# First feed-forward product with both parts of the activations in one 512-column matmul

## The chip, the cores and the metric

The kernel runs on one core of one Trainium2 chip. A core has a matrix engine (TensorE; PE in the profile, its weight loads PEld), a vector engine (VectorE, DVE), an activation engine (ScalarE, ACT), GpSimd (POOL) and a queue that issues DMA transfers (SyncE, SP). The metric is the device time of one launch in microseconds (us). Matmuls write to PSUM, which is divided into banks of 512 float32 columns on 128 partitions.

## The reference

Two layers over 256 tokens of width 1024. Each layer normalises its input, runs three token mixers and adds their gated sum; then comes the feed-forward block, which is what this case is about:

```python
def hybrid_layer(x, ...):
    h = rms_norm(x, g_mix)
    z = h @ w_in
    ...
    x = x + (g_a * o_a + g_b * o_b + g_c * o_c) @ w_out
    h = rms_norm(x, g_ffn)
    x = x + jnp.square(jax.nn.relu(h @ w_ff1)) @ w_ff2
    return x
```

`w_ff1` is 1024 x 4096 and `w_ff2` 4096 x 1024, all in float32.

## The kernel before

**Products in three parts.** A float32 number is split exactly into two float32r numbers, a high and a low part. A product is then three float32r matmuls that add up in PSUM: high by high, high by low and low by high. Weights arrive by DMA in pieces of 128x1024 into one of five `raw` buffers; `piece` (L153, L154) splits a piece: ScalarE copies `raw` to `hi`, VectorE subtracts and writes `lo`. There are four `hi` and four `lo` buffers; the second feed-forward product takes its pieces (named `hi2`, `lo2`) from a second ring of five larger buffers.

**The feed-forward block.** It goes in 16 groups per layer, each with 256 of the 4096 hidden channels: two halves u = 0, 1 of 128 channels. `ff1(gi)` loads and splits two pieces of `w_ff1`, one for each half. `gemm_b` (L163 to L165) then makes, for each half and each of 8 row tiles k of 128 input channels, three matmuls of 256 columns (the 256 tokens): `hi` by `h2`, `hi` by `l2`, `lo` by `h2`, where `h2` and `l2` are the high and low parts of the transposed, scaled input. Both halves lie side by side in one PSUM bank. The pool `mm` has two banks, so two groups can be under way. Then ScalarE takes the relu out of the bank (L888), squares it into `rh` (L890), VectorE computes the same square with full precision (L891) and subtracts to get the low part `rl` (L892).

`acc_pass` makes the second product: for each group 24 matmuls of 512 columns (L171 to L173, tiles `f`) into four banks that hold the sums of the whole layer. In program text the first product of group gi + 1 stands ahead of the second product of group gi; the second products of the last three groups are held back to the end of the layer.

**The start of the block.** `transposed` (L203 to L208) turns the residual stream into `h2` and `l2`, 128x128 chunk by chunk: TensorE transposes (`n2t`), ScalarE scales into `h2` (L207), VectorE subtracts into `l2` (L208). The first group takes the row tiles k in two halves, 0 to 3 and 4 to 7, in the order in which they arrive.

**What sets the order.** The order on each engine is decided when the program is built: a scheduler orders the instructions by priority (the order of the text, corrected by hand in places) and by when it expects their inputs and buffers to be ready. On the chip each engine works through its own list in that order, and an instruction that has to wait holds up everything behind it on its engine.

Of the kernel before, what the change touches and what calls it, by code (L numbers as in the profile page):

```python
# [8 lines left out]
F32 = mybir.dt.float32  # L9
# [7 lines left out]
P = 128  # L17
# [14 lines left out]
# column offsets of the packed per-partition parameters  # L32
# [9 lines left out]
# row-broadcast gains of the rotary dims: [g, g with halves swapped]  # L42
# [16 lines left out]
# w_in: columns read with tokens on the output's partitions, then those with channels there  # L59
# [6 lines left out]
# the mixers' steps in the order of their data, and by urgency  # L66
# [19 lines left out]
def trunk_kernel(ctx: ExitStack, tc: tile.TileContext, A, out, depth=DEPTH):  # L86
# [54 lines left out]
    def piece(src, k, ring=0, half=0):  # L141
        """a piece [128, k, n] of a weight, split exactly into two float32r parts"""
        n = src.shape[-1]
        r = raw(src, n)
        if ring == 0:
            hi = wp.tile([P, 1024], R32, tag="hi", name="hi", bufs=WB)[:, :n]
            lo = wp.tile([P, 1024], R32, tag="lo", name="lo", bufs=WB)[:, :n]
        else:
            if half == 0:
                ring2[0] = (ap_.tile([P, 2048], R32, tag="big", name="hi2", bufs=BIG),  # L150
                            ap_.tile([P, 2048], R32, tag="big", name="lo2", bufs=BIG))
            hi, lo = (t[:, half * 1024:half * 1024 + n] for t in ring2[0])
        act(hi, r, AF.Copy)  # L153
        tt(out=lo, in0=r, in1=hi.bitcast(F32), op=ALU.subtract)  # L154
        return tuple(t.rearrange("p (k n) -> p k n", k=k) for t in (hi, lo))
# [3 lines left out]
    def gemm_b(ps, wh, wl, ah, al, ks, first=True, last=True):  # L159
        """ps[channel, token] += w^T a^T"""  # L160
# [5 lines left out]

    def gemm_a(ps, ah, al, wh, wl, ks, first=True, last=True):
        """ps[token, channel] += a w"""
# [10 lines left out]
    def rsqrt(v, p, n, name):  # L179
        """1/sqrt(v) of a positive [p, n] tile"""  # L180
# [18 lines left out]
    def transposed(src, b, g, hh, hl, name, c0):  # L199
        """columns c0 ... c0 + 3 (of 128) of src [128 tokens, 1024] -> block b of (src^T * g), split"""  # L200
# [3 lines left out]
        for c in range(c0, c0 + 4):  # L204
            pc = pt[:, (c - c0) * P:(c - c0 + 1) * P]
            hc = hh[:, c, b * P:(b + 1) * P]
            act(hc, pc, AF.Copy, scale=g[:, c:c + 1])  # L207
            stt(out=hl[:, c, b * P:(b + 1) * P], in0=pc, scalar=g[:, c:c + 1], in1=hc.bitcast(F32),  # L208
                op0=ALU.mult, op1=ALU.subtract)
# [5 lines left out]
    def normed(src, b, r, grow, hh, hl, name):  # L215
        """src [128 tokens, 1024] -> columns of block b of (src * r * g)^T, split"""
# [10 lines left out]
    def sumsq_row(b, name, v):  # L227
        """mean square of x's rows in block b, plus eps"""
# [11 lines left out]
    def rope(X, n, half, ct, st, name, eng=None):  # L240
        """rotate the first 2*half columns of X [p, n, d] in place; ct, st [p, 2*half]"""
# [12 lines left out]
    def layer(l):  # L254
# [20 lines left out]

        hB = lambda t: (lambda k: t[k] if isinstance(t, list) else t[:, k, :])
# [4 lines left out]
        hh = ap_.tile([P, 8, T], R32, tag="hh", name="hh", bufs=2)  # L281
        hl = ap_.tile([P, 8, T], R32, tag="hl", name="hl", bufs=2)
        grow = raw(bass.AP(tensor=A["gmix"].tensor, offset=A["gmix"].offset + l * D, ap=[[0, P], [1, D]]), D)
        vs = stat(2, "n1v")
        for b in range(NB):
            now = tc.cur_priority
            if l > 0 and b == 0:
                # block 0 goes before the last products of the block 1 of the layer before
# [11 lines left out]
        # rotary tables times the gains of the rotated dims  # L300
# [20 lines left out]
        def part_a(i):  # L321
            """accumulators and weights; the products are added block by block"""
# [9 lines left out]
        # channel-major part  # L332
        def take(*names):
            """one or two tiles, in one bank"""
# [21 lines left out]
        def a_products():  # L356
            """the first two parts; block 0 goes ahead"""
# [70 lines left out]
        def compress_kv():  # L428
# [13 lines left out]
            for xi, (wn, pe, w2) in enumerate((("ck1", "pek", "ck2"), ("cv1", "pev", "cv2"))):  # L442
# [11 lines left out]
                # four column groups of the array at a time; their sums are added by the next product  # L454
# [41 lines left out]
        def compress_scores():  # L496
            """all heads at once: order (block, pair, group, position)"""
# [31 lines left out]
        oh = ol = None  # L529

        def softmax_unit(pS, n, gate, name):
            """pS [128, n, keys] scores, a bank -> P^T [128 keys, 4 x 128 queries]"""
# [5 lines left out]
            # the negated masked scores and their minimum  # L538
# [24 lines left out]
        def nsa_attention(jp, o):  # L563
            """heads 2 jp, 2 jp + 1 of both groups"""
            po = psum("po", "nO")

            for b, js in ((0, (0, 1)), (1, (0,)), (1, (1,))):
# [3 lines left out]
                # the groups' products take turns: halves of the array that work at the same time  # L571
# [26 lines left out]
        def mla_attention(jp, o):  # L598
            """heads 4 jp ... 4 jp + 3"""
# [35 lines left out]
        def gemm32(ps, b, w, ks, c0, n):  # L635
            """ps[token, channel] = c_q or c_kv times w, a plain float32 product"""
# [6 lines left out]
        def low_rank_norm():  # L643
# [7 lines left out]
            # eps * (mean(c_q^2) + eps): per-token scale that the norm of c_q moves into the heads' norm  # L651
# [9 lines left out]
        def rotary_keys():  # L661
            krs = stat(2, "krs")
            # rotary part of the keys, shared by the heads
# [155 lines left out]
        def gated(m, c2):  # L819
            """column tiles 2 c2, 2 c2 + 1 of mixer m's projection, gated; the last of the three sums them"""  # L820
# [12 lines left out]
            if len(done[c2]) == 3:  # L833
                if mh is None:
                    mh = ap_.tile([P, 8, T], R32, tag="hh", name="mh", bufs=2)
                    ml = ap_.tile([P, 8, T], R32, tag="hl", name="ml", bufs=2)
                c = 2 * c2
                split(mh[:, c:c + 2].rearrange("p c t -> p (c t)"), ml[:, c:c + 2].rearrange("p c t -> p (c t)"), g)

        oh = ap_.tile([P, 8, T], R32, tag="hh", name="oh", bufs=2)  # L840
        ol = ap_.tile([P, 8, T], R32, tag="hl", name="ol", bufs=2)
# [11 lines left out]
        def acc_pass(po4, held, ah, al, nk, b, ns=(0, 1)):  # L853
            """add the products of the held row tiles to the accumulators of token block b"""
# [7 lines left out]
        h2 = ap_.tile([P, 8, T], R32, tag="hh", name="h2", bufs=2)  # L862
        l2 = ap_.tile([P, 8, T], R32, tag="hl", name="l2", bufs=2)
        for b in range(NB):
            if b == 0:
                acc_pass(po4, held, mh, ml, 8, b)
            for n in range(2):
# [4 lines left out]
                transposed(x[:, b], b, K("gffn"), h2, l2, "n2t", 4 * n)  # L872
# [5 lines left out]
        def ff1(gi):  # L878
            ps = psum("mm", "ff1")
            ws = [piece(A["ff1"][l, 2 * gi + u], 8) for u in range(2)]  # L880
            # the first group takes the channels in the order in which they arrive
            for k0, k1 in ((0, 4), (4, 8)) if gi == 0 else ((0, 8),):
                for u in range(2):
                    wh, wl = ws[u]
                    gemm_b(ps[:, u * T:(u + 1) * T], lambda k: wh[:, k, :], lambda k: wl[:, k, :], hB(h2), hB(l2),
                           [(k, k) for k in range(k0, k1)], first=(k0 == 0 and (u == 0 or gi > 0)), last=(k1 == 8 and (u == 1 or gi > 0)))
            r = s2([P, 512], "r")
            act(r, ps, AF.Relu)  # L888
            rhf, rlf = pa("rh", R32), pa("rl", R32)
            act(rhf, r, AF.Square)  # L890
            stt(out=r, in0=ps, scalar=0.0, in1=r, op0=ALU.max, op1=ALU.mult)  # L891
# [38 lines left out]
def _lay(w, k, n):  # L930
    """[L, k*128, c*n] -> [L, c, 128, k*n]: chunks of n columns, contiguous per partition"""
# [4 lines left out]
def _rowsplit(w, k):  # L936
    """[L, K, n] -> [L, K/(128 k), 128, k*n]: chunks of k row tiles"""
# [118 lines left out]
```

## Time and profile before

| what | value |
|---|---|
| time, median of 3 runs | 940.52 us (935.05 to 941.61) |
| span of the profiled execution | 932.9 us |
| the profiled execution's own time | not listed apart; the three runs lie 2.2 to 8.7 us above its span |
| TensorE busy | 907.7 us, 97% of the span |
| VectorE, ScalarE busy | 642.6 us (69%), 538.4 us (58%) |
| mean granted TensorE clock | 0.996 of full speed |
| feed-forward block, layer 1 and layer 2 | about 292 to 475 us and 747 to 930 us of the span |

The span runs from the first to the last instruction of one execution that the hardware profiler recorded. The duration of a single matmul in it (283 ns for 256 columns) is longer than the distance from one start to the next, because matmuls overlap; what a stream of them costs is read from the starts. The granted clock is given as a share of full speed: 1.00 is 2.4 GHz and 0.50 is 1.2 GHz.

### The profile page before, as it was taken

What the parts mean: (1) busy time and instruction counts of PE and PEld (TensorE: products, weight loads), DVE (VectorE), ACT (ScalarE), POOL (GpSimd) and SP (SyncE); (2) the same over time, 40 slices, a digit from 0 to 9 for tenths busy, and PEclk for the clock granted to TensorE, in tenths of its full rate; (3) what the DMA queues carried; (4) which work ended last, traced back from release to release, by engine and by line L of the source; (5) the groups of instructions that cost most, each with busy time, mean ns of one, the idle gap of its engine ahead of it and who ended that gap; (6) DMA issues with size and microseconds to landing.
All of it is one profiled execution on the core that took longest, in us unless ns stands there. A gap on an engine that the chain in (4) does not pass through costs nothing.

```text
span 932.9 us, 16104 instructions
## 1 busy us (share of the span) xinstructions
PE 907.7 (97%) x6214; PEld 804.6 (86%) x6214; DVE 642.6 (69%) x1431; ACT 538.4 (58%) x987; POOL 26.8 (3%) x80
## 2 busy tenths in 40 slices
PE   3999999999999999999999999999999999999998
PEld 3899888689989899999878988877999799999996
DVE  4589899775687655555476989979657785555552
ACT  3566656897456644444245575769865575444430
POOL 3210000000000000000001000000000000000000
PEclk9899999999999999999999999999999999999999
DMA  5644732224565665555444453225435476555521
GB/s 197 250 158 137 239 119 79 77 105 167 173 208 178 233 196 188 184 194 185 125 153 171 159 199 135 85 80 178 142 104 190 155 267 207 184 188 189 186 91 46
DMA packets 43133, 151.55 MB, mean 162 GB/s; under 512 B 4784, under 2 KB 5680, under 8 KB 43056
## 3 DMA queue, kind: packets, MB, share of 16 engines
q1 hardware_dynamic: 43056, 150.52, 48.2%
q8 instruction: 49, 0.80, 0.3%
q14 instruction: 28, 0.23, 0.1%
HBM read 149.45 MB, written 1.05 MB: 161 GB/s over the span
## 4 chain that ended last, share of the span: by engine, by line
PE 89%; DVE 4%; DMA 3%; ACT 2%; POOL 1%; issue 1%; SPq 0%; DVEq 0%; ACTq 0%
PE psB L163 7%; PE psB L165 7%; PE psB L164 7%; PE f L173 6%; PE f L171 6%; PE f L172 6%; PE ff L164 6%; PE ff L163 6%; PE ff L165 6%; PE wo L164 3%; PE wo L163 3%; PE wo L165 2%; PE nS L576 2%; DVE lo L154 2%; PE psA L172 2%; PE psA L171 2%
## 5 line engine op out<-in xcount | busy, mean ns | idle before, releaser
L154 DVE TENSOR_TENSOR lo<-raw,hi 128x1024 fp32r<-128x1024 f32 (+1 forms) x266 | 317.5, 1209 | 179.0 <-ACT hi L153 140.8
L153 ACT ACTIVATE hi<-raw 128x1024 fp32r<-128x1024 f32 (+1 forms) x266 | 274.7, 1048 | 267.2 <-DMA raw<-in_ff_dram 93.6
L163 PE MATMUL psB<-hh,hi 128*128 128x256 f32 x592 | 172.4, 292 | 1.4 <-ACT ug L749 1.4
L165 PE MATMUL psB<-hh,lo 128*128 128x256 f32 x592 | 170.2, 289 | 0.0
L164 PE MATMUL psB<-hl,hi 128*128 128x256 f32 x592 | 169.5, 287 | 0.0
L165 PE MATMUL ff<-h,lo 128*128 128x256 f32 x512 | 144.5, 283 | 0.0
L163 PE MATMUL ff<-h,hi 128*128 128x256 f32 x512 | 144.5, 283 | 0.0
L164 PE MATMUL ff<-l,hi 128*128 128x256 f32 x512 | 144.3, 283 | 0.0
L163 PEld LDWEIGHTS psB<-hh,hi 128*128 128x128 f32 x592 | 113.1, 191 | 8.2 <-issue 4.4
L165 PEld LDWEIGHTS psB<-hh,lo 128*128 128x128 f32 x592 | 112.8, 191 | 3.0 <-issue 2.6
L164 PEld LDWEIGHTS psB<-hl,hi 128*128 128x128 f32 x592 | 113.1, 191 | 0.3
L758 DVE SCALAR_TENSOR_TENSOR ca<-upad,cols,ca 128x256 f32<-128x256 f32 x240 | 103.6, 477 | 0.4
L173 PE MATMUL f<-hi,rl 128*128 128x512 f32 x256 | 101.2, 395 | 0.5 <-DVE rl L892 0.5
L171 PE MATMUL f<-hi,rh 128*128 128x512 f32 x256 | 101.1, 395 | 0.0
L172 PE MATMUL f<-lo,rh 128*128 128x512 f32 x256 | 101.0, 395 | 0.0
L164 PEld LDWEIGHTS ff<-l,hi 128*128 128x128 f32 x512 | 98.0, 192 | 1.1
L163 PEld LDWEIGHTS ff<-h,hi 128*128 128x128 f32 x512 | 97.9, 191 | 1.2
L165 PEld LDWEIGHTS ff<-h,lo 128*128 128x128 f32 x512 | 98.0, 192 | 0.0
L173 PEld LDWEIGHTS f<-hi,rl 128*128 128x128 f32 x256 | 48.0, 188 | 13.0 <-DVE rl L892 1.6
L171 PEld LDWEIGHTS f<-hi,rh 128*128 128x128 f32 x256 | 48.1, 188 | 10.2
L172 PEld LDWEIGHTS f<-lo,rh 128*128 128x128 f32 x256 | 48.0, 188 | 10.3
L171 PE MATMUL psA<-hi,hh 128*128 128x512 f32 (+1 forms) x96 | 36.4, 381 | 6.9 <-ACT hi L153 6.9
(279 smaller groups left out, 1425.1 us busy)
## 6 DMA issues: line engine op xcount, KB each, us to landing
raw<-in_ff_dram SPq DMA_DIRECT2D x128, 512.0 KB, 4.0
raw<-in_wB_dram SPq DMA_DIRECT2D x74, 512.0 KB, 4.0
raw<-in_wA_dram SPq DMA_DIRECT2D x16, 512.0 KB, 4.4
raw<-in_w_out_dram SPq DMA_DIRECT2D x16, 512.0 KB, 3.5
raw<-in_wo_nsa_dram SPq DMA_DIRECT2D x8, 512.0 KB, 4.8
raw<-in_wo_mla_dram SPq DMA_DIRECT2D x8, 512.0 KB, 4.0
raw<-in_wconv_dram SPq DMA_DIRECT2D x8, 512.0 KB, 3.7
raw<-in_wA_dram SPq DMA_DIRECT2D x8, 312.0 KB, 5.3
```

The costliest lines, as they stand in the source:

```text
L153: act(hi, r, AF.Copy)
L154: tt(out=lo, in0=r, in1=hi.bitcast(F32), op=ALU.subtract)
L163: mm(ps, lhsT=wh(kw), rhs=ah(ka), start=(first and i == 0), stop=False)
L164: mm(ps, lhsT=wh(kw), rhs=al(ka), start=False, stop=False)
L165: mm(ps, lhsT=wl(kw), rhs=ah(ka), start=False, stop=(last and i == n - 1))
L171: mm(ps, lhsT=ah(ka), rhs=wh(kw), start=(first and i == 0), stop=False)
L172: mm(ps, lhsT=ah(ka), rhs=wl(kw), start=False, stop=False)
L173: mm(ps, lhsT=al(ka), rhs=wh(kw), start=False, stop=(last and i == n - 1))
L576: mm(pS[g].rearrange("p (h z k) -> p h z k", h=nj, z=2)[:, i], lhsT=qTn[gs, 2 * jp + j, b * P:(b + 1) * P], rhs=kTn[gs, :, 0:nk], start=Tr ...
L758: stt(out=ca[:, i], in0=upad[:, i, k:k + T], scalar=K("wdw", 31 * i + k), in1=ca[:, i], op0=ALU.mult, op1=ALU.add)
```

## The change

`h2` and `l2` become one tile `h2` of shape [128, 8, 2, 256], so that for each row tile the high and the low part lie side by side as 512 columns (the other activation tiles get the same layout, and are read as before). A new function `gemm_p` makes two matmuls for each row tile where `gemm_b` made three: `hi` by both parts in one matmul of 512 columns, and `lo` by the high part with 256 columns, which adds into the left half of the result. A half of a group now fills a whole PSUM bank: the left 256 columns hold hi by high plus lo by high, the right 256 columns hi by low. So one group takes both banks of the pool `mm`. The left and right columns are summed afterwards: ScalarE copies the left ones to `r`, VectorE adds the right ones, once for each half; the relu and the square follow on VectorE from `r`, and ScalarE copies the square into `rh`. The comments that the diff also drops are not shown.

```diff
+    def gemm_p(ps, wh, wl, a, ks, first=True, last=True):
+
+        n = len(ks)
+        for i, (kw, ka) in enumerate(ks):
+            mm(ps, lhsT=wh(kw), rhs=a[:, ka].rearrange("p s t -> p (s t)"), start=(first and i == 0), stop=False)
+            mm(ps[:, :T], lhsT=wl(kw), rhs=a[:, ka, 0], start=False, stop=(last and i == n - 1))
+
...
-            hc = hh[:, c, b * P:(b + 1) * P]
+            hc = h[:, c, 0, b * P:(b + 1) * P]
             act(hc, pc, AF.Copy, scale=g[:, c:c + 1])
-            stt(out=hl[:, c, b * P:(b + 1) * P], in0=pc, scalar=g[:, c:c + 1], in1=hc.bitcast(F32),
+            stt(out=h[:, c, 1, b * P:(b + 1) * P], in0=pc, scalar=g[:, c:c + 1], in1=hc.bitcast(F32),
                 op0=ALU.mult, op1=ALU.subtract)
...
+        def pair(name):
+
+            return ap_.tile([P, 8, 2, T], R32, tag="hp", name=name, bufs=2)
+
...
-        h2 = ap_.tile([P, 8, T], R32, tag="hh", name="h2", bufs=2)
-        l2 = ap_.tile([P, 8, T], R32, tag="hl", name="l2", bufs=2)
+        h2 = pair("h2")
...
         def ff1(gi):
-            ps = psum("mm", "ff1")
             ws = [piece(A["ff1"][l, 2 * gi + u], 8) for u in range(2)]
-            # the first group takes the channels in the order in which they arrive
+            pss = [psum("mm", "ff1") for _ in range(2)]
+
             for k0, k1 in ((0, 4), (4, 8)) if gi == 0 else ((0, 8),):
                 for u in range(2):
                     wh, wl = ws[u]
-                    gemm_b(ps[:, u * T:(u + 1) * T], lambda k: wh[:, k, :], lambda k: wl[:, k, :], hB(h2), hB(l2),
-                           [(k, k) for k in range(k0, k1)], first=(k0 == 0 and (u == 0 or gi > 0)), last=(k1 == 8 and (u == 1 or gi > 0)))
+                    gemm_p(pss[u], lambda k: wh[:, k, :], lambda k: wl[:, k, :], h2,
+                           [(k, k) for k in range(k0, k1)], first=(k0 == 0), last=(k1 == 8))
             r = s2([P, 512], "r")
-            act(r, ps, AF.Relu)
+            for u in range(2):
+                rt = r[:, u * T:(u + 1) * T]
+                act(rt, pss[u][:, :T], AF.Copy)
+                tt(out=rt, in0=pss[u][:, T:], in1=rt, op=ALU.add)
             rhf, rlf = pa("rh", R32), pa("rl", R32)
-            act(rhf, r, AF.Square)
-            stt(out=r, in0=ps, scalar=0.0, in1=r, op0=ALU.max, op1=ALU.mult)
+            stt(out=r, in0=r, scalar=0.0, in1=r, op0=ALU.max, op1=ALU.mult)
+            act(rhf, r, AF.Copy)
             tt(out=rlf, in0=r, in1=rhf.bitcast(F32), op=ALU.subtract)
```

The built order moves at the start of each layer's feed-forward block. The lists below are of layer 1; layer 2 has the same pattern. A row gives the line, the operation, the tile written, the tiles read and the shape; the numbers tell buffers of one name apart.

TensorE before, in the second half of group 0 (`ff1_3484`, weights `hi_3487` and `hi_3493`); `ff1_3570` is group 1:

```order
L163 MATMUL ff1_3484<-h2_3326,hi_3487 128x256
L163 MATMUL ff1_3570<-h2_3326,hi_3573 128x256
L164 MATMUL ff1_3570<-l2_3327,hi_3573 128x256
L165 MATMUL ff1_3570<-h2_3326,lo_3574 128x256
L163 MATMUL ff1_3570<-h2_3326,hi_3573 128x256
L164 MATMUL ff1_3484<-l2_3327,hi_3487 128x256
L165 MATMUL ff1_3484<-h2_3326,lo_3488 128x256
L164 MATMUL ff1_3570<-l2_3327,hi_3573 128x256
```

The same engine with the change, from row tile 6 of group 0 (`ff1_3492` and `ff1_3493` are its two halves) to the first products of group 1 (`ff1_3566`):

```order
L171 MATMUL ff1_3492<-h2_3323,hi_3482 128x512
L172 MATMUL ff1_3492<-h2_3323,lo_3483 128x256
L171 MATMUL ff1_3493<-h2_3323,hi_3488 128x512
L172 MATMUL ff1_3493<-h2_3323,lo_3489 128x256
L171 MATMUL ff1_3492<-h2_3323,hi_3482 128x512
L172 MATMUL ff1_3492<-h2_3323,lo_3483 128x256
L171 MATMUL ff1_3493<-h2_3323,hi_3488 128x512
L172 MATMUL ff1_3493<-h2_3323,lo_3489 128x256
L171 MATMUL ff1_3566<-h2_3323,hi_3556 128x512
L172 MATMUL ff1_3566<-h2_3323,lo_3557 128x256
```

Before, products of group 1 stand among those of group 0; with the change group 1 follows only behind the last product of group 0, since it writes to the same two banks.

ScalarE before, from the last chunk of `h2` to the end of the work on group 0 (`hi2_3742` is a piece for the second product of group 1, `hi_3675` the first piece for group 2):

```order
L207 ACTIVATE h2_3326<-n2t_3467,cols_82 128x128 x4
L153 ACTIVATE hi2_3742<-raw_3740 128x1024
L153 ACTIVATE hi_3675<-raw_3673 128x1024
L153 ACTIVATE hi2_3742<-raw_3746 128x1024
L888 ACTIVATE r_3545<-ff1_3484 128x512
L232 ACTIVATE n2_q_3553,n2_ss_3554<-x_74 128x512
L890 ACTIVATE rh_3547<-r_3545 128x512
```

ScalarE with the change, over the same stretch (`hi_3646` is the first piece for group 2):

```order
L214 ACTIVATE h2_3323<-n2t_3463,cols_82 128x128 x4
L153 ACTIVATE hi2_3702<-raw_3700 128x1024
L153 ACTIVATE hi_3646<-raw_3644 128x1024
L900 ACTIVATE r_3526<-ff1_3492 128x256
L900 ACTIVATE r_3526<-ff1_3493 128x256
L239 ACTIVATE n2_q_3537,n2_ss_3538<-x_74 128x512
L239 ACTIVATE n2_q_3546,n2_ss_3547<-x_74 128x512
L239 ACTIVATE n2_q_3537,n2_ss_3538<-x_74 128x512
L239 ACTIVATE n2_q_3546,n2_ss_3547<-x_74 128x512
L153 ACTIVATE hi_3652<-raw_3650 128x1024
L904 ACTIVATE rh_3531<-r_3526 128x512
```

Two splits still stand ahead of the first read of the banks; the third has moved behind it, and `rh` now comes behind four sums of squares and one split.

VectorE before, over the same stretch:

```order
L208 SCALAR_TENSOR_TENSOR l2_3327<-n2t_3467,cols_82,h2_3326 128x128 x2
L154 TENSOR_TENSOR lo2_3743<-raw_3740,hi2_3742 128x1024
L154 TENSOR_TENSOR lo_3676<-raw_3673,hi_3675 128x1024
L154 TENSOR_TENSOR lo2_3743<-raw_3746,hi2_3742 128x1024
L891 SCALAR_TENSOR_TENSOR r_3545<-ff1_3484,r_3545 128x512
```

VectorE with the change:

```order
L215 SCALAR_TENSOR_TENSOR h2_3323<-n2t_3463,cols_82,h2_3323 128x128 x2
L154 TENSOR_TENSOR lo2_3703<-raw_3700,hi2_3702 128x1024
L154 TENSOR_TENSOR lo_3647<-raw_3644,hi_3646 128x1024
L901 TENSOR_TENSOR r_3526<-ff1_3492,r_3526 128x256
L901 TENSOR_TENSOR r_3526<-ff1_3493,r_3526 128x256
L903 SCALAR_TENSOR_TENSOR r_3526<-r_3526 128x512
```

The two additions that empty the banks stand behind two splits. From group 1 on the pattern of both engines is regular: a split of a first-product piece stands ahead of each half's copy and addition. The DMA queue keeps the order of its transfers, but for one exchange of neighbours in each layer.

## Rows read from the trace of the kernel before

**Rows 1.** The page, busy time, share of the span and instructions of each engine.

```profile
PE 907.7 (97%) x6214; PEld 804.6 (86%) x6214; DVE 642.6 (69%) x1431; ACT 538.4 (58%) x987; POOL 26.8 (3%) x80
```

**Rows 2.** TensorE's waits, 285 to 475 us: total, times, longest.

```profile
PE f L173 <- DVE rl L892: 0.5, 1, 0.5
```

**Rows 3.** Timeline of TensorE in one group: start, duration, instruction.

```profile
380.07 0.28 PE L164 MATMUL ff<-l,hi 128*128 128x256 f32 x1
...
383.91 0.39 PE L171 MATMUL f<-hi,rh 128*128 128x512 f32 x1
...
389.48 0.28 PE L163 MATMUL ff<-h,hi 128*128 128x256 f32 x1
```

**Rows 4.** Timeline of ScalarE and VectorE in the next group.

```profile
392.44 1.06 ACT L153 ACTIVATE hi<-raw 128x1024 fp32r<-128x1024 f32 x1 [1.44 <-PE ff L164]
...
396.28 0.58 ACT L888 ACTIVATE r<-ff 128x512 f32<-128x512 f32 x1
...
398.29 0.69 DVE L892 TENSOR_TENSOR rl<-r,rh 128x512 fp32r<-128x512 f32 x1
...
400.78 2.36 DVE L154 TENSOR_TENSOR lo<-raw,hi 128x1024 fp32r<-128x1024 f32 x2 [1.80 <-PE f L172]
```

**Rows 5.** Groups by form: count, busy us, mean ns, idle before.

```profile
L154 DVE TENSOR_TENSOR lo<-raw,hi 128x1024 fp32r<-128x1024 f32 x258 | 311.2, 1222 | 176.9 <-ACT hi L153 138.8 <-PE f L172 37.7
L153 ACT ACTIVATE hi<-raw 128x1024 fp32r<-128x1024 f32 x258 | 269.3, 1058 | 264.3 <-DMA raw<-in_ff_dram 93.6 <-PE ff L164 45.1 <-PE psB L164 40.4
...
L891 DVE SCALAR_TENSOR_TENSOR r<-ff,r 128x512 f32<-128x512 f32 x32 | 22.1, 691 | 4.1 <-ACT rh L890 4.1
L890 ACT ACTIVATE rh<-r 128x512 fp32r<-128x512 f32 x32 | 20.3, 634 | 0.8
...
L770 DVE TENSOR_TENSOR ca<-ca,cmu 128x256 f32<-128x256 f32 x8 | 3.3, 414 | 0.9 <-PE cmu L767 0.9
...
L385 ACT ACTIVATE vsw<-psA 128x256 f32<-128x256 f32 x4 | 1.5, 384 | 0.0
```

**Rows 6.** Timeline at the start of the block, layer 1.

```profile
296.85 0.34 DVE L208 SCALAR_TENSOR_TENSOR l<-n2t,cols,h 128x128 fp32r<-128x128 f32 x1
...
297.63 0.35 DVE L208 SCALAR_TENSOR_TENSOR l<-n2t,cols,h 128x128 fp32r<-128x128 f32 x1 [0.44 <-ACT h L207]
...
298.62 2.01 ACT L153 ACTIVATE hi<-raw 128x1024 fp32r<-128x1024 f32 x2 [1.02 <-DMA raw<-in_ff_dram]
299.71 1.23 DVE L154 TENSOR_TENSOR lo<-raw,hi 128x1024 fp32r<-128x1024 f32 x1 [1.73 <-ACT hi L153]
...
303.81 0.39 PE L171 MATMUL f<-hi,rh 128*128 128x512 f32 x1
...
304.95 0.50 PE L173 MATMUL f<-hi,rl 128*128 128x512 f32 x1 [0.52 <-DVE rl L892]
```

**Rows 7.** Timeline at the start of the block, layer 2.

```profile
752.41 0.35 DVE L208 SCALAR_TENSOR_TENSOR l<-n2t,cols,h 128x128 fp32r<-128x128 f32 x1 [0.43 <-ACT h L207]
...
754.23 1.23 DVE L154 TENSOR_TENSOR lo<-raw,hi 128x1024 fp32r<-128x1024 f32 x1 [1.47 <-ACT hi L153]
...
758.58 0.39 PE L171 MATMUL f<-hi,rh 128*128 128x512 f32 x1
```

**Rows 8.** Windows of 1 us: busy (x) of PE, PEld, DVE, ACT, POOL, PEclk, DMA.

```profile
20.00:21.00 1.00, 0.00 (x0) 0.00 (x0) 0.00 (x0) 0.00 (x0) 0.00 (x0) 1.00 0.78 166
21.00:22.00 1.00, 0.00 (x0) 0.00 (x0) 0.00 (x0) 0.00 (x0) 0.00 (x0) 0.64 1.01 369
...
27.00:28.00 1.00, 1.00 (x4) 0.81 (x4) 1.00 (x3) 0.78 (x2) 0.00 (x0) 0.50 0.81 258
28.00:29.00 1.00, 1.00 (x6) 0.82 (x5) 0.74 (x2) 1.00 (x2) 0.00 (x0) 0.95 0.96 344
```

**Rows 9.** Timeline of TensorE around the same stretch.

```profile
18.61 0.30 PE L173 MATMUL psA<-hi,hl 128*128 128x312 f32 x1
24.69 0.79 PE L171 MATMUL psA<-hi,hh 128*128 128x512 f32 x1 [5.77 <-ACT hi L153]
```

More of the change, by code (lines that the diff above doesn't have):

```diff
@@ L197, in rsqrt, with transposed @@
         return y
-    def transposed(src, b, g, hh, hl, name, c0):
+    def transposed(src, b, g, h, name, c0):
         pt = psum("pt", name)
@@ L278, in layer @@
         col = lambda ap: ap.rearrange("p (n o) -> p n o", o=1)
-        hh = ap_.tile([P, 8, T], R32, tag="hh", name="hh", bufs=2)
-        hl = ap_.tile([P, 8, T], R32, tag="hl", name="hl", bufs=2)
+        hp = pair("hp")
+        hh, hl = hp[:, :, 0], hp[:, :, 1]
         grow = raw(bass.AP(tensor=A["gmix"].tensor, offset=A["gmix"].offset + l * D, ap=[[0, P], [1, D]]), D)
@@ L834, in gated @@
                 if mh is None:
-                    mh = ap_.tile([P, 8, T], R32, tag="hh", name="mh", bufs=2)
-                    ml = ap_.tile([P, 8, T], R32, tag="hl", name="ml", bufs=2)
+                    mp = pair("mp")
+                    mh, ml = mp[:, :, 0], mp[:, :, 1]
                 c = 2 * c2
-                split(mh[:, c:c + 2].rearrange("p c t -> p (c t)"), ml[:, c:c + 2].rearrange("p c t -> p (c t)"), g)
-        oh = ap_.tile([P, 8, T], R32, tag="hh", name="oh", bufs=2)
-        ol = ap_.tile([P, 8, T], R32, tag="hl", name="ol", bufs=2)
+                split(mh[:, c:c + 2], ml[:, c:c + 2], g.rearrange("p (c t) -> p c t", c=2))
+        op = pair("op")
+        oh, ol = op[:, :, 0], op[:, :, 1]
         steps = {"a": a_products, "a0": a_compressed, "a1": a_keys, "a2": a_queries, "qk": nsa_qk, "glu": glu, "lr": low_rank, "lrn": low_rank_norm, "ckv": compress_kv, "csc": compress_scores,
@@ L871, in layer @@
                 stt(out=xs, in0=po4[b][n], scalar=0.5, in1=xs, op0=ALU.mult, op1=ALU.add)
-                transposed(x[:, b], b, K("gffn"), h2, l2, "n2t", 4 * n)
+                transposed(x[:, b], b, K("gffn"), h2, "n2t", 4 * n)
         po4 = [[psum("at", "f0"), psum("at", "f1")], [psum("po", "f2"), psum("ch", "f3")]]
```

## The prediction

> **What bounds the kernel now.** I read the page first. TensorE is busy for 97% of the span [rows 1]: anything gained has to shorten its stream, and any wait put into it is paid in full. Then its waits inside the feed-forward block: in 190 us of layer 1 there is a single one, 0.5 us [rows 2]. The block is a gapless run of matmuls, so I price it by distances between starts, not by the durations in the groups. From 380.07 to 383.91 stand 32 products of 256 columns [rows 3]: 0.120 us each. From 383.91 to 389.48 stand the 24 products of 512 columns: 0.232 us each. A group is 48 x 0.120 + 24 x 0.232 = 11.33 us. ScalarE and VectorE have slack: a group needs four splits at 1.06 and 1.22 us [rows 5] and a little more, some 5.4 and 6.3 us out of 11.3.
>
> **The gain on TensorE.** A row tile of a half took three products of 256 columns, 0.360 us; it now takes one of 512 and one of 256, 0.232 + 0.120 = 0.352 us. The columns streamed are the same 768; what is saved is the fixed part of one product. There are 2 layers x 16 groups x 16 = 512 such steps, so 4.1 us at most. The halved instruction count deceives: a 512-column product costs nearly twice a 256-column one. No row shows the two sizes taking turns. Bounds: the saving per step may be the whole fixed part of a 256-column product, 0.120 less 0.107 (256 columns at 2.4 GHz) = 0.013 us, 6.9 us in all, or nothing. I take 0.008 us, since both rows are of this very block. A new group is then 16 x 0.352 + 5.57 = 11.20 us, 0.13 us shorter.
>
> The Trainium skill, "TensorE: Matmul & The Clock Gate", section "Back-to-back issue gap", puts the fixed part at about 2.5 ns for an isolated warm product; by it all 512 steps would save an estimated 1.3 us instead of 4.1. The rows show about 13 ns at 256 columns, and they decide.
>
> **The regular groups: the drain is covered.** Count from the first product of a group. Half 0 ends at 2.8 us. ScalarE then makes the split that waits for it (before, too, a split waits there for TensorE, at 392.44 [rows 4] against the group's start at 389.48), until 3.9, and copies half a bank. The nearest row of the same kind, a 256-column copy out of PSUM, takes 0.38 us [rows 5]: until 4.3. VectorE has the low split until 5.1, and adds; the nearest row, a 256-column operation with a PSUM operand, takes 0.41 us: the first bank is free at 5.5. The next group wants it at 11.2, since the 24 products of the second matmul lie between. Half 1 ends at 5.6, its split at 6.7, its low split at about 8.0, its addition at 8.4; it is wanted at 14. Then square (0.69), copy into `rh` (0.63) and `rl` (0.69) end at about 10.5; they are wanted at 16.8, and VectorE's next work, which waits for TensorE's last use of a `lo2` buffer (400.78 in [rows 4]), comes at 11.3. Per group ScalarE swaps 0.58 + 0.63 for 2 x 0.38 + 0.63 us and VectorE gains 0.83. All of that is hidden. If the cover of the second product were gone, the drain would stand bare; that is so at the start of the block.
>
> **The start of the block: a new wait.** Before, group 1 had a bank of its own, and its products stood among those of group 0, filling the time in which the last chunks of `h2` and `l2` come one by one. Now group 1 needs both banks of group 0, and no second product lies between. Layer 1 [rows 6]: the chunk of row tile 6 is ready at 297.19, that of tile 7 at 297.98; two halves at 0.35 follow, so group 0 ends at 298.7. The first bank is read only behind two splits on each engine. The first of them waits for its transfer until 298.62; both `hi` end at 300.63. VectorE starts its first `lo` at 299.71 and, at 1.22 each, ends the second at 302.15; with the addition the bank is free at about 302.5. TensorE stands for 3.8 us. The 16 steps of group 1 end at 302.5 + 5.63 = 308.1. Before, the second product began at 303.81 and lost 0.52 us at its third matmul: in effect 304.3. The loss is 3.8 us. `rh` and `rl` of group 0 are in time: two copies, four sums of squares (0.63 each, as the row of the same size on ScalarE), a split and the copy bring `rh` to 305.7, and `rl` follows a low split, to about 307.
>
> Layer 2 [rows 7]: last chunk at 752.76, group 0 ends at 753.5; second `lo` at 754.23 + 2 x 1.22 = 756.7, bank free at 757.1; group 1 ends at 762.7, where the second product began at 758.58 before. The loss is 4.1 us. Both losses already hold the shorter steps of groups 0 and 1.
>
> **The end of the block.** Group 14 and group 15 stand back to back. By the count above the banks are free at 5.5 and 8.4 us, and group 15 wants them at 5.6 and 8.45. I put 0.2 us per layer, ends 0 and 1.2 (one split late).
>
> **The clock.** A pause of 3.5 to 3.8 us can cost clock as well. The kernel's first stretch shows it: the last product ends at 18.91, and the granted clock falls from 1.00 (2.4 GHz) to 0.50 (1.2 GHz) in the window 21 to 22, 2.4 us into the pause. TensorE resumes at 24.69 and gets the full clock back at about 28.1 [rows 8, 9]: 3.4 us of work at half speed, 1.7 us lost. The 0.52 us wait of [rows 6] cost no clock. Here each pause outlasts 2.4 us, so I expect a fall in most cases, but perhaps not in both layers. Ends per layer: 0, and 2.8 us, if a low stretch as long as that one (6.8 us) overlapped the pause by only 1.2 us. I take 1.25 us per layer, nearer to the row than to none.
>
> **Sum** against the span of 932.9 us: 28 regular groups x 0.13 = -3.6; starts +3.8 and +4.1; ends of the block +0.4; clock +2.5: together +7.2, a span of 940.1. The median of the runs lies 7.6 us above the span; I shift it by the same 7.2: 947.7 us, 0.8% longer. About 1% is what a measurement of this kernel can tell from no change, so the forecast counts as no change, on its slow edge.
>
> **Rivals.**
> - *No lost clock, or a larger gain on the steps.* Without the clock term the sum is +4.7 (945.2); with 0.013 us per step as well, +2.3 (942.8). For it: the pause is only 1.1 to 1.4 us longer than what passed before the fall in [rows 8]. I count these into the same case as the forecast, 0.70 together with it.
> - *Slower by over 1%.* The mechanism is the pause at the start. The bank waits for a split that waits for a transfer; the low clock then lasts as long as in [rows 8]. Clock at its upper end gives +10.3 (950.8); if the 512-column product saves nothing beside the 256-column one, +10.8 (951.3); both, +14. It decides at +9.4. For it: the full price of the clock alone is enough, and ScalarE was waiting for a transfer at 298.62. Against: layer 2 has the same pattern with its transfers on time. Chance 0.24.
> - *The pause does not come.* If the drain found the splits already done, group 1 would follow at once: the sum is -4.1 from the steps and some +1 from the late chunks, about 937. The built order stands against it: both splits are ahead of the copy, and the second reuses the buffer that group 0's first half has just read. Chance 0.04.
> - *A wait in every group.* If the drain slipped behind the next group's start, each of 28 groups would wait; at 2.3 us (one more pair of splits, 1.06 + 1.22) that is 64 us, about 1012. Against it: 5.7 us of slack for bank 0. Chance 0.02. The Trainium skill, same page, section "A second HAM failure mode: psum-queue depth-cycling", says that cycling through PSUM banks can pause TensorE between groups often enough to make its clock swing; that is this rival. No row before shows a pause between groups.
>
> **How the numbers follow.** Likeliest is the forecast, 947.7. The range goes from 941 (the large gain and no lost clock, less 2 us of scatter) to 953 (clock at its upper end, plus 2 us). Faster by over 1% (below 931.1) needs a gain that the steps cannot give: 0.02. Slower by over 1% (above 949.9): the second and fourth rivals, 0.26. The rest is 0.72.
>
> **What would show it.** In the profile after: 0.352 us from one 512-column product to the next and 11.20 us from group to group; one wait of 3 to 4 us of the first product of group 1, ended by VectorE's addition, in each layer; the granted clock at 0.50 for some us behind it; no wait in groups 2 to 13; more busy time on VectorE by about 32 x 0.83 = 27 us. I am wrong if steps are not 0.352 us, if the additions wait in regular groups, or if other work is found for TensorE in the pause.

## The result and the profile after

The changed kernel takes 945.97 us (median of 6 runs, 941.72 to 948.41), the kernel before 937.78 us (median of 6 runs, 934.61 to 941.61). The ratio is 1.0086, 95% interval 1.0057 to 1.0114: 8.1 us slower, where 7.2 us slower had been forecast.

The profiled execution is the longest of the six (948.41 us, span 946.3 us). First its page: busy time and the groups that are new.

```profile
PE 913.7 (97%) x5702; PEld 784.4 (83%) x5702; DVE 667.2 (71%) x1495; ACT 540.0 (57%) x1019; POOL 26.6 (3%) x80
...
L171 PE MATMUL ff<-h,hi 128*128 128x512 f32 x512 | 186.2, 404 | 7.5 <-DVE r L901 6.6
...
L172 PE MATMUL ff<-h,lo 128*128 128x256 f32 x512 | 145.0, 284 | 0.0
```

TensorE has 512 products fewer than in [rows 1] and is busy no shorter. VectorE has 24.6 us more. The 6.6 us of idle time behind `DVE r` is what to look for. The waits of TensorE, 285 to 480 us (total, times, longest):

```profile
PE ff L171 <- DVE r L901: 3.1, 1, 3.1
PE ff L171 <- DVE h L215: 0.4, 1, 0.4
```

In the whole block of layer 1 the drain is waited for once; layer 2 has the same two lines, with 3.4 for 3.1. The one wait of [rows 2] is gone. Where the new one stands (timeline of TensorE; in brackets the idle time and what ended it):

```profile
292.94 0.40 PE L171 MATMUL ff<-h,hi 128*128 128x512 f32 x1
...
298.45 0.50 PE L171 MATMUL ff<-h,hi 128*128 128x512 f32 x1 [0.43 <-DVE h L215]
...
299.94 0.28 PE L172 MATMUL ff<-h,lo 128*128 128x256 f32 x1
303.36 0.79 PE L171 MATMUL ff<-h,hi 128*128 128x512 f32 x1 [3.15 <-DVE r L901]
...
304.17 0.63 PE L171 MATMUL ff<-h,hi 128*128 128x512 f32 x1
...
304.81 0.63 PE L171 MATMUL ff<-h,hi 128*128 128x512 f32 x1
...
311.77 0.40 PE L178 MATMUL f<-hi,rh 128*128 128x512 f32 x1
```

299.94 is the last product of group 0, 303.36 the first of group 1. Its duration, 0.79 us against 0.40 for the same instruction at 292.94, already tells of a slow clock. ScalarE and VectorE in the same pause:

```profile
299.52 2.00 ACT L153 ACTIVATE hi<-raw 128x1024 fp32r<-128x1024 f32 x2 [0.72 <-DMA raw<-in_ff_dram]
300.61 2.36 DVE L154 TENSOR_TENSOR lo<-raw,hi 128x1024 fp32r<-128x1024 f32 x2 [1.43 <-ACT hi L153]
301.43 0.64 ACT L900 ACTIVATE r<-ff 128x256 f32<-128x256 f32 x2
302.89 0.75 DVE L901 TENSOR_TENSOR r<-ff,r 128x256 f32<-128x256 f32 x2
```

The drain is 0.3 to 0.4 us per half on each engine. It comes 1.2 us late on ScalarE and then 1.3 us late again on VectorE, because two weight splits stand ahead of it in each list. Layer 2 has the same chain, headed by a split that waits 0.98 us for its transfer (ScalarE, then TensorE):

```profile
762.88 2.00 ACT L153 ACTIVATE hi<-raw 128x1024 fp32r<-128x1024 f32 x2 [0.98 <-DMA raw<-in_ff_dram]
...
766.72 0.77 PE L171 MATMUL ff<-h,hi 128*128 128x512 f32 x1 [3.42 <-DVE r L901]
```

The windows with the granted clock (the sixth figure behind the comma, not counting those in brackets: PEclk) show what follows:

```profile
300.00:303.00 3.00, 0.22 (x2) 0.00 (x0) 2.39 (x3) 3.00 (x7) 0.00 (x0) 0.93 0.86 280
303.00:306.00 3.00, 2.64 (x8) 2.25 (x9) 2.60 (x10) 3.00 (x9) 1.53 (x5) 0.50 0.71 235
306.00:309.00 3.00, 3.00 (x11) 2.60 (x10) 2.45 (x3) 1.04 (x2) 0.00 (x0) 0.50 0.64 202
309.00:312.00 3.00, 3.00 (x17) 2.58 (x16) 1.65 (x2) 2.19 (x4) 0.00 (x0) 0.93 0.82 240
...
560.00:565.00 5.00, 5.00 (x24) 4.81 (x23) 3.29 (x23) 2.01 (x6) 0.00 (x0) 0.50 1.00 342
...
766.00:770.00 4.00, 3.28 (x10) 2.80 (x11) 3.61 (x12) 4.00 (x10) 0.00 (x0) 0.60 0.84 254
770.00:774.00 4.00, 4.00 (x25) 3.52 (x24) 3.44 (x5) 2.56 (x4) 0.00 (x0) 0.97 0.67 172
```

In layer 1 the clock is at its lower level (0.50, 1.2 GHz) from about 302.6 to 309.4; from 303.36 on that is 6.0 us of work. A step takes 0.64 us there (304.17 to 304.81), which is just its 768 columns at 1.2 GHz, and 0.35 us at the full clock: 1.8 times as long and not twice. So 6.0 us at the lower level lose 2.7 us. In layer 2, by the last two rows, the clock is low for 3.4 us behind the pause: 1.5 us lost. The row 560 to 565 is another low stretch, in the mixers of layer 2, which this change does not touch; more on it below.

The regular groups, by the first products of three successive groups and the steps of one:

```profile
373.32 0.39 PE L171 MATMUL ff<-h,hi 128*128 128x512 f32 x1
373.55 0.28 PE L172 MATMUL ff<-h,lo 128*128 128x256 f32 x1
373.67 0.40 PE L171 MATMUL ff<-h,hi 128*128 128x512 f32 x1
...
374.73 0.40 PE L171 MATMUL ff<-h,hi 128*128 128x512 f32 x1
...
384.57 0.39 PE L171 MATMUL ff<-h,hi 128*128 128x512 f32 x1
...
390.12 0.40 PE L178 MATMUL f<-hi,rh 128*128 128x512 f32 x1
...
395.72 0.39 PE L171 MATMUL ff<-h,hi 128*128 128x512 f32 x1
```

From 373.32 to 374.73 are four steps, 0.353 us each. Groups last 11.25 us (373.32 to 384.57) and 11.15 us (384.57 to 395.72) in turn, 11.20 on average, against 11.33 in [rows 3]. The difference lies in the first product: its 16 steps take 5.65 us in one group and 5.55 in the next (384.57 to 390.12, 0.347 each), while the 24 `f` products take 5.60 in both.

To find where the time went, I split each span at four kinds of starts on TensorE:

| stretch | before, us | after, us | difference |
|---|---|---|---|
| start to first `ff` product, layer 1 | 291.87 | 292.94 | +1.07 |
| first `ff` to first `f` product, layer 1 | 11.94 | 18.83 | +6.89 |
| first to last `f` product, layer 1 | 171.53 | 169.06 | -2.47 |
| last `f` of layer 1 to first `ff` of layer 2 | 271.31 | 275.21 | +3.90 |
| first `ff` to first `f`, layer 2 | 11.93 | 17.90 | +5.97 |
| first to last `f`, layer 2 | 169.86 | 168.03 | -1.83 |
| last `f` to the end | 4.44 | 4.37 | -0.07 |

The spans differ by 13.4 us. The four stretches of the two blocks and the end make up 8.5 us of it, close to the 8.1 us of the medians. The rest, 5.0 us, lies ahead of the two blocks, in the mixers. Up to 3.4 us of it is the low stretch at 560 us, 6.8 us long, which is not the change's doing (e5 below). The profiled execution of before had no such stretch.

### The profile page after: what moved, and what is told of

It is laid out like the page before. It is cut to its first block, busy times and chain, and to the rows that moved or that the text cites. A ratio compares the mean times of both kernels' runs of the same rounds, so it can differ in the third digit from the quotient of the medians.

```text
span 946.3 us, 15170 instructions
## 1 busy us (share of the span) xinstructions
PE 913.7 (97%) x5702; PEld 784.4 (83%) x5702; DVE 667.2 (71%) x1495; ACT 540.0 (57%) x1019; POOL 26.6 (3%) x80
## 4 chain that ended last, share of the span: by engine, by line
PE 86%; DVE 5%; DMA 4%; ACT 2%; issue 1%; POOL 1%; SPq 0%; DVEq 0%; ACTq 0%
PE ff L171 12%; PE psB L163 7%; PE psB L165 7%; PE psB L164 7%; PE f L178 6%; PE f L180 6%; PE f L179 6%; PE ff L172 6%; DVE lo L154 3%; PE wo L164 2%; PE wo L163 2%; PE wo L165 2%; PE nS L587 2%; PE psA L178 2%; PE psA L179 2%; PE psA L180 2%
## 5 line engine op out<-in xcount | busy, mean ns | idle before, releaser
L171 PE MATMUL ff<-h,hi 128*128 128x512 f32 x512 | 186.2, 404 | 7.5 <-DVE r L901 6.6
L163 PE MATMUL psB<-hp,hi 128*128 128x256 f32 x592 | 173.3, 293 | 1.7 <-ACT ug L760 1.7
L165 PE MATMUL psB<-hp,lo 128*128 128x256 f32 x592 | 171.3, 291 | 0.0
L164 PE MATMUL psB<-hp,hi 128*128 128x256 f32 x592 | 170.3, 288 | 0.0
L163 PEld LDWEIGHTS psB<-hp,hi 128*128 128x128 f32 x592 | 113.9, 192 | 8.4 <-issue 4.4
L165 PEld LDWEIGHTS psB<-hp,lo 128*128 128x128 f32 x592 | 113.8, 193 | 3.0 <-issue 2.6
L164 PEld LDWEIGHTS psB<-hp,hi 128*128 128x128 f32 x592 | 113.9, 192 | 0.3
L904 ACT ACTIVATE rh<-r 128x512 fp32r<-128x512 f32 x32 | 20.2, 632 | 54.8 <-DVE r L903 54.8
L178 PE MATMUL psA<-hi,hp 128*128 128x512 f32 (+1 forms) x96 | 36.9, 386 | 6.3 <-ACT hi L153 6.3
L179 PE MATMUL psA<-lo,hp 128*128 128x512 f32 (+1 forms) x96 | 36.9, 384 | 1.0 <-DVE lo L154 1.0
```

Source lines behind the costliest of these rows:

```text
L163: mm(ps, lhsT=wh(kw), rhs=ah(ka), start=(first and i == 0), stop=False)
L164: mm(ps, lhsT=wh(kw), rhs=al(ka), start=False, stop=False)
L165: mm(ps, lhsT=wl(kw), rhs=ah(ka), start=False, stop=(last and i == n - 1))
L171: mm(ps, lhsT=wh(kw), rhs=a[:, ka].rearrange("p s t -> p (s t)"), start=(first and i == 0), stop=False)
L178: mm(ps, lhsT=ah(ka), rhs=wh(kw), start=(first and i == 0), stop=False)
L179: mm(ps, lhsT=ah(ka), rhs=wl(kw), start=False, stop=False)
```

## The experiments

Theory: the whole loss is one bare pause per layer before group 1, since group 0 holds both banks of the pool and two splits stand ahead of its drain, plus the clock that falls behind the pause; the gain is 0.13 us per group. Rivals: the loss lies in the drain's extra vector work or in the new layout; the wait depends on the queues and not on the banks; the clock falls for another reason; the gain is not that of the wide product. All eight kernels start from the changed one. Four were run on one chip beside 34 runs of before (median 937.79 us), four on one chip beside 24 runs (937.03 us).

### e1: the old form in groups 0 and 1

```diff
+            if gi < 2:
+                ps = psum("mm", "ff1")
...
+                        gemm_b(ps[:, u * T:(u + 1) * T], lambda k: wh[:, k, :], lambda k: wl[:, k, :], hB(h2[:, :, 0]), hB(h2[:, :, 1]),
...
+                act(r, ps, AF.Relu)
...
```

> Groups 0 and 1 of each layer take the old form (one bank, three 256-column products per step, the old drain), groups 2 to 15 the new one; the pair layout stays. Bare-pause theory (the loss is one pause per layer before group 1, because group 0 holds both banks, and the clock that falls behind it): no pause on TensorE between group 0 and group 1, from the first ff product to the first f product 11.9 us in both layers as before (18.8 and 17.9 after), and 13 to 14 groups per layer keep 0.13 us each, 3.4 to 3.6 us in all: 0.996 of before, about 934 us. Rival, the loss lies in the pair layout or in the drain's extra work on VectorE (27 us): most of it stays, 1.005 or more. Rival, the group's gain is not real: 1.000.

Measured: 934.97 us, ratio 0.9982 (0.9961 to 1.0002). From the first `ff` to the first `f` product 11.93 us in both layers; groups of 11.15 and 11.25 us. No wait for a drain in `ff`; the wait at the start of the second product is there, as in [rows 6]. The profile puts it down to the small `n_v` that VectorE makes behind `rl`; in the timeline `rl`, which this product reads, ends at about the same time:

```profile
PE f L180 <- DVE n_v L241: 0.7, 1, 0.7
```

The loss goes away with the form of two groups out of 16, though 14 groups keep the new layout and the vector work. First to last `f` products are 1.37 and 1.41 us shorter than before. The gain of 0.996 was a little too high an expectation; the interval ends just above 1.

### e2: group 1 in other banks

```diff
-            pss = [psum("mm", "ff1") for _ in range(2)]
+            pss = [psum("pt" if gi == 1 else "mm", "ff1") for _ in range(2)]
```

> The new form everywhere, but group 1 writes to the two banks that the transposes of the norm have left. The drain's place behind the weight splits is as in the changed kernel. Bare-pause theory: no wait for a drain at the block's start, the clock stays up, all 16 groups keep their gain: 11.7 to 12 us from the first ff to the first f product, 0.996 of before, about 934 us, 12 us less than the changed kernel. Rival, what hurts is where the drain stands in the queues of ScalarE and VectorE, whatever the banks: the wait moves to group 2 and 1 to 3 us per layer stay lost, 1.000 to 1.005. Rival, layout or vector work: 1.005 or more.

Measured: 934.44 us, 0.9969 (0.9947 to 0.9991). The two splits still stand ahead of the drain, which ScalarE and VectorE reach when TensorE is already at work on group 1:

```profile
300.83 0.64 ACT L900 ACTIVATE r<-ff 128x256 f32<-128x256 f32 x2
...
302.29 0.75 DVE L901 TENSOR_TENSOR r<-ff,r 128x256 f32<-128x256 f32 x2
```

No `ff` product waits. What is late next is the copy into `rh` (waits of TensorE, 288 to 480 us):

```profile
PE f L178 <- ACT rh L904: 0.4, 1, 0.4
```

So 12.39 and 12.40 us to the first `f` product, a little more than the expected 12, against 11.94 before and 18.83 after. One line of bank choice removes the loss: with a free bank, the place of the drain in the lists costs a wait of 0.4 us (0.7 to 0.8 us by the start of e8) instead of 3 to 4.

### e3: the drain ahead of the splits

```diff
+        def later(*a, **k):
+            with tc.issue_after(drained[0].ins), tc.issue_after(drained[1].ins):
+                return piece(*a, **k)
...
-            ws = [piece(A["ff1"][l, 2 * gi + u], 8) for u in range(2)]
+            ws = [(later if 2 < 2 * gi + u < 6 else piece)(A["ff1"][l, 2 * gi + u], 8) for u in range(2)]
...
+            if gi == 0:
+                drained[:] = da, dv
...
+            held.append([(2 * gi + u, u) + (later if gi < 2 else piece)(A["ff2"][l, 2 * gi + u], 1, ring=int(gi < NG - tail + 2), half=u) for u in range(2)])
```

Here `da` and `dv` are the copy and the addition of the second half.

> The weight splits that stood ahead of group 0's drain on ScalarE and VectorE (the second piece of group 1, the pieces of group 2 and the first two pairs of the second product's weights) go behind it; banks as in the changed kernel. Bare-pause theory: the pause before group 1 falls from 3.4 and 3.7 us to 1 to 1.5 us (a copy of 0.32, an add of 0.38 and the steps between them), 2 to 2.5 us less per layer; if the clock then stays up, a further 3.0 and 1.7 us: 1.000 to 1.004 of before, against 1.0086 for the change. Rival, the drain itself takes as long as the pause: pause over 3 us, 1.008.

Measured: 933.57 us, 0.996 (0.9942 to 0.9978), better than expected. TensorE's waits, 288 to 480 us:

```profile
PE ff L172 <- DVE lo L154: 0.6, 1, 0.6
PE ff L171 <- DVE r L907: 0.2, 1, 0.2
```

With both banks still held by group 0, the pause is 0.2 us, not 3.15, and not the 1 to 1.5 us that I had added up. The halves of group 0 end one after the other, and the first half is drained while TensorE still makes the last step of the second (from 299.93):

```profile
299.78 0.39 ACT L906 ACTIVATE r<-ff 128x256 f32<-128x256 f32 x1 [1.10 <-PE ff L172]
...
300.20 0.42 DVE L907 TENSOR_TENSOR r<-ff,r 128x256 f32<-128x256 f32 x1 [1.13 <-ACT r L906]
...
300.68 0.50 PE L171 MATMUL ff<-h,hi 128*128 128x512 f32 x1 [0.22 <-DVE r L907]
```

The clock stayed at 1.00 through both block starts. A second wait, 0.6 us, is of my making: the second piece of group 1 was put behind the drain too. From first `ff` to first `f`: 13.16 and 13.17 us. The theory has to be put more exactly: the banks alone do not make the pause; two splits ahead of the drain do, when no bank is free. Either remedy is enough.

### e4: the pause filled with products

```diff
+            if gi == 1:
+                fill = psum("pt", "fill")
+                with tc.issue_after(last0[0].ins):
+                    for i in range(13):
+                        mm(fill, lhsT=ws[0][0][:, i % 8, :], rhs=h2[:, i % 8].rearrange("p s t -> p (s t)"),
+                           start=(i == 0), stop=(i == 12))
```

> 13 products of 512 columns (3.0 us by the 0.23 us of one), written to a bank that nobody reads, stand between group 0 and group 1; nothing else changes. Clock theory: the pause in the useful work stays at 3.4 to 3.7 us, but the granted clock does not fall behind it (6.8 us at half speed in layer 1 and 3.4 us in layer 2 after the change), which gives back 3.0 and 1.7 us: 1.003 to 1.004 of before, 941 us. Rival, the clock falls for another reason (the thin transposes ahead of the block): the low stretch stays and the time is that of the changed kernel, 1.0086.

Measured: 943.64 us, 1.0055 (1.0036 to 1.0074). The timeline of TensorE in layer 1:

```profile
301.97 0.28 PE L172 MATMUL ff<-h,lo 128*128 128x256 f32 x1
302.09 3.17 PE L897 MATMUL fill<-h,hi 128*128 128x512 f32 x13
305.10 0.39 PE L171 MATMUL ff<-h,hi 128*128 128x512 f32 x1
```

Group 1 starts 3.13 us after the start of the last product of group 0, nearly as late as after the change (3.42), but its first product takes 0.39 us instead of 0.79, and the windows have the full clock:

```profile
305.00:308.00 3.00, 3.00 (x19) 2.60 (x18) 2.59 (x9) 3.00 (x7) 0.92 (x1) 1.00 0.80 299
308.00:311.00 3.00, 3.00 (x19) 2.58 (x18) 3.00 (x5) 2.78 (x5) 2.88 (x5) 1.00 0.59 203
```

From first `ff` to first `f`: 15.75 us (18.83 after) and 16.92 us (17.90 after; there a wait of 0.9 us remained behind the filler, and group 1 started 4.18 us after the last product of group 0, against 3.70). That gives back 4.1 us in the trace; the ratios differ by 0.0031, 2.9 us, with wide intervals, and less than was expected. From the first product of group 1 to the first `f` product layer 1 takes 5.64 us here and 8.41 after the change: 2.8 us are the clock's, near the 2.7 worked out from the windows. The clock fell because TensorE stood still, and what the clock lost, 4.2 us in both layers, is a third of the 12.9 us at the two starts.

### e5: e2 with three products of 256 columns

```diff
-            mm(ps, lhsT=wh(kw), rhs=a[:, ka].rearrange("p s t -> p (s t)"), start=(first and i == 0), stop=False)
+            mm(ps[:, :T], lhsT=wh(kw), rhs=a[:, ka, 0], start=(first and i == 0), stop=False)
+            mm(ps[:, T:], lhsT=wh(kw), rhs=a[:, ka, 1], start=False, stop=False)
```

> As e2 (group 1 in the transposes' banks, no pause), but the 512-column product is two of 256 columns with the same weights, one into each half of the bank; the drain stays that of the change. Step theory: the gain is the 0.13 us per group of the wide product (16 groups per layer, 4 us in all), so the period of a group goes back from 11.20 to 11.33 us and the time to 1.000 to 1.001 of before, about 938 us. Rival, the gain comes from the drain or the layout: the time of e2 stays, 0.997.

Measured: 936.59 us, 0.9993 (0.9973 to 1.0014). The timeline of TensorE, first products of two successive groups:

```profile
377.32 0.28 PE L171 MATMUL ff<-h,hi 128*128 128x256 f32 x1
...
388.65 0.28 PE L171 MATMUL ff<-h,hi 128*128 128x256 f32 x1
```

11.33 us again, as before. First to last `f` product takes 171.02 and 169.76 us, against 168.96 and 167.80 in e2: the wide product is worth 2.06 and 1.96 us per layer there, which is nearly all that e2 gains in that stretch; the rest is the wait of [rows 2], which is gone in both. The kernel has the new layout and the new drain (VectorE busy 665.5 us, 642.6 before) and is no slower than before: layout and vector work cost nothing measurable.

This kernel also answers for the low clock in the mixers. Its windows there (PEclk as above):

```profile
480.00:485.00 5.00, 3.16 (x13) 2.04 (x11) 2.71 (x5) 1.54 (x2) 0.00 (x0) 1.00 0.89 339
485.00:490.00 5.00, 4.95 (x21) 4.31 (x22) 3.01 (x6) 1.27 (x3) 1.07 (x5) 0.66 0.72 210
```

Beside the one at the start that every trace has [rows 8], such a stretch of 3.4 or 6.8 us stands in the mixers of the traces of e1 to e7, at 129, 485 to 492, 551 or 582 us, and in none of e8's or of the execution of before shown ahead. With half of such stretches taken off (an estimate), the part from the last `f` of layer 1 to the first `ff` of layer 2 takes 270.3 to 272.5 us in all ten traces, 271.3 before and 271.8 after. The mean clock of the runs of before goes from 0.989 to 0.997 (58 runs). So the low stretch comes and goes from run to run, with and without the change; what starts it is not shown.

### e6: the new form in group 0 alone

```diff
+            if gi > 0:
+                ps = psum("mm", "ff1")
...
```

The rest as in e1.

> Only group 0 of each layer takes the new form with its two banks; groups 1 to 15 have the old one. Bare-pause theory: the whole loss of the change and next to none of its gain: 17.5 to 19 us from the first ff to the first f product in both layers against 11.9, the clock low behind the pause, groups of 11.33 us: 1.010 to 1.014 of before, 947 to 951 us. Rival, the loss is spread over the groups (VectorE's 27 us): 1.000 to 1.002.

Measured: 947.06 us, 1.0091 (1.0058 to 1.0124), a little under the expected 1.010. Groups 1 to 15 last 11.33 us. TensorE's waits, 288 to 480 us, and the windows behind the pause:

```profile
PE ff L163 <- DVE r L915: 3.4, 1, 3.4
PE ff L171 <- DVE h L215: 0.4, 1, 0.4
```

```profile
303.00:306.00 3.00, 0.94 (x4) 0.95 (x5) 2.96 (x6) 3.00 (x10) 0.67 (x2) 0.57 0.91 317
306.00:309.00 3.00, 3.00 (x16) 3.00 (x15) 2.65 (x10) 2.63 (x5) 0.78 (x4) 0.50 0.65 208
```

18.83 and 19.22 us to the first `f` product: one group per layer in the new form brings the whole loss of the change. With e1 this puts the loss at the two starts and nowhere else. Here the clock was low for 6.8 us in both layers.

### e7: the drain first, group 1's second piece left in place

e3 with `later` used for the first product's pieces only where `gi == 2`.

> As e3 (two banks as in the change, group 0's drain ahead of splits), but the second piece of group 1 is split where the scheduler puts it; only the pieces of group 2 and of the second product go behind the drain. Bare-pause theory: a pause of 0.9 to 2 us (one split of 1.06 and 1.23 us may be ahead), no wait of 0.6 us for the second piece: 12.5 to 14 us to the first f product against 13.2 in e3, 0.995 to 0.998 of before.

Measured: 934.03 us, 0.9971 (0.9944 to 0.9998). The wait for the second piece is gone; TensorE's waits, 288 to 480 us:

```profile
PE ff L171 <- DVE r L907: 0.5, 1, 0.5
```

12.44 and 12.43 us to the first `f` product (13.16 in e3), just below what was expected. The pause is 0.5 us in both layers, less than the expected 0.9 to 2, and the clock stayed up behind it.

### e8: e2 and e7 together

Both edits, nothing else.

> e2 and e7 together: group 1 in the other banks, and the pieces of group 2 and of the second product behind group 0's drain. Nothing to wait for at the block's start: 11.7 to 12.1 us to the first f product (12.4 in e2, where the first f product waited 0.36 us for the drain's copy), 0.995 to 0.997 of before, 933 to 935 us. Rival, what is moved behind the drain comes too late for the first f products: a new wait for their weights, 0.998 or more.

Measured: 930.96 us, 0.9932 (0.9904 to 0.9959), the fastest of all, faster than both kernels and than expected. There is no wait of TensorE from 288 to 480 us or in the block of layer 2. The timeline, first `ff` and first `f` product of layer 1:

```profile
291.42 0.40 PE L171 MATMUL ff<-h,hi 128*128 128x512 f32 x1
...
303.11 0.40 PE L178 MATMUL f<-hi,rh 128*128 128x512 f32 x1
```

11.69 us, and 11.61 in layer 2, below the 11.94 and 11.93 of before. In the blocks and the end the trace is 4.9 us shorter than before (0.25 and 0.32 at the starts, 2.42 and 1.80 from first to last `f`, 0.06 at the end). The ratio, 6.4 us, is higher than that, but its interval reaches down to 3.8 us.

## Why the prediction was right, and where a term was off

The forecast was 0.8% slower, by a pause at each block's start that outweighs the shorter steps; that is what happened, for the reasons given. Point by point:

- **Steps.** 0.352 us and 11.20 us per group were forecast. The group is 11.20 on average, but not in the way forecast: its steps take 0.353 us in one group and 0.347 in the next, 0.350 on average, and the 24 `f` products 5.60 us where 5.57 had been taken over from before. e5 shows that the wide product alone makes the gain. First to last `f` shows -2.47 and -1.83, together 4.3, where 28 x 0.13 = 3.6 stood in the sum. In layer 1 the wait of [rows 2] is in it: before, the 24 `f` products of group 0 take 6.38 us (303.81 to 310.19), against 5.58 in the groups behind and 5.59 after, so the wait was worth 0.8 us. That leaves 3.5 for the steps. (The largest possible gain of the steps was given as 6.9 us; 512 x 0.0133 is 6.8.) The Trainium skill, "TensorE: Matmul & The Clock Gate", section "Back-to-back issue gap", has a fixed part of about 2.5 ns for an isolated product at the full clock. Here 0.13 us over 16 steps is 8 ns for each product saved, three times that.
- **Regular groups.** No wait was forecast, none is there; VectorE got 24.6 us more work where 27 had been worked out.
- **Start of the block.** Without the clock, 4.3 us were forecast from first `ff` to first `f` in layer 1 (the 3.8 of the sum had 0.5 taken off for the wait of [rows 2]) and 4.1 in layer 2. Measured: 6.89 - 2.7 = 4.2 us, and 5.97 - 1.5 = 4.5 us. In layer 1 two errors met: the pause was shorter than worked out (3.15 against 3.8 us), and group 0 took 0.4 us longer, among it the 0.43 us wait for a chunk of `h`. The chain named (transfer, two splits, copy, addition) is the one in the timeline. One argument was wrong: that layer 2 has its transfers on time. The kernel before shows it already, in a line that [rows 7] leave out:

```profile
753.14 2.96 ACT L153 ACTIVATE hi<-raw 128x1024 fp32r<-128x1024 f32 x3 [0.76 <-DMA raw<-in_ff_dram]
```

After the change the split that heads the chain waited 0.98 us for its transfer, until 762.88. Had it been on time, the drain and with it group 1 would have come up to 1 us earlier, by an estimate from the timeline.

- **End of the block.** 0.2 us per layer was forecast. TensorE has no such wait in either layer.
- **The clock: the step that was mis-sized.** "I take 1.25 us per layer", between 0 and 2.8. It cost 2.7 us in layer 1, close to the upper end, and 1.5 us in layer 2: 4.2 us instead of 2.5. In layer 1 the clock fell at 302.6, 0.8 us before TensorE resumed at 303.36; in layer 2 it fell at about 766.8, as TensorE resumed, and stayed low half as long. The price per us was a little too high, since work at the lower level was taken to run at half speed and here it takes 1.8 times as long. The mean clock points the same way: 0.994 (before, 34 runs), 0.989 (after, 6 runs).
- **Together:** 4.2 + 4.5 + 4.2 - 3.5 - 0.8 - 0.1 = 8.5 us in the trace (the starts, the clock, the steps, the lost wait, the end), and 8.1 us in the medians, against 7.2 forecast. The larger clock loss was partly met by the end of the block and the lost wait. That the total came so near is in part luck.
- **Rivals.** *Slower by over 1%* had the right mechanism and was near: in layer 1 the price of the clock came out close to its upper end. *No lost clock* is refuted by the windows and by e4. *The pause does not come* did not happen, but e3 and e7 show how close it was: with the splits behind the drain it is 0.2 to 0.5 us. *A wait in every group* did not occur; the Trainium skill, same page, section "A second HAM failure mode: psum-queue depth-cycling", describes pauses between groups with a swinging clock, and here the clock swung at the one pause per layer and at no group in between.

## What to carry to other kernels

A step that takes a whole PSUM pool for one group removes the cover of its drain at that one place where no other work lies between two groups; look there first, and not at the average group. The price of a pause on a full TensorE is the pause plus the clock behind it, which was half as much again here (4.2 us beside 8.7). It was cured twice over: by one line that gives the second group two banks that stand idle, and by letting the drain go ahead of splits that are not yet needed; with both, a change that lost 0.9% gains 0.7%.

## What the runs showed of the hardware

- A pause of 3.15 us took the clock down for 6.8 us and one of 3.42 us for 3.4 us in the same execution; in e6 two pauses of 3.4 us took it down for 6.8 us each. Waits of 0.2 to 0.9 us at the same places (e3, e4, e7) did not. What decides between the two lengths is not shown.
- A 512-column product with a 256-column one behind it takes 0.353 us as a pair in one group and 0.347 in the next, about the sum of the two spacings read from uniform stretches (0.232 and 0.120). At the lower clock the pair takes 0.64 us, 1.8 times as long: no fixed part shows there beside its 768 columns at 1.2 GHz.
- The groups' length alternates between 11.15 and 11.25 us wherever the wide product is used in the regular groups (after, e1 to e4, e7, e8), and is a steady 11.33 where it is not (before, e5, e6). The 0.1 us lies in the first product alone (5.55 and 5.65 us; `f` takes 5.60 in both). What makes it alternate stays open.
